# Modulation rows 2 to 8 summed along the row on VectorE, in a hybrid encoder layer on one core

## The chip, the cores and the metric

The kernel runs on one core of a Trainium2 chip. The metric is the device time of one execution in microseconds; the median of several executions is compared.

## The reference

One layer of an encoder is computed for two request groups that share all weights: 1024 prompt rows and 32 sample rows, 1056 in all, of 1024 features each. Everything is fp32.

```python
mod = (silu(c) @ w_ada + b_ada).reshape(B, 9, D_MODEL)[:, None]     # one c per group
modulate = lambda h, k: h * (1.0 + mod[:, :, 3*k + 1]) + mod[:, :, 3*k]
gate = lambda k: 1.0 + mod[:, :, 3*k + 2]
f = swiglu(modulate(x, 0), ffn1_w1, ffn1_w3, ffn1_w2)               # 1024 -> 2816 -> 1024
x = layer_norm(ALPHA * x + 0.5 * gate(0) * f, ln_g[0], ln_b[0])
proj = modulate(x, 1) @ w_in                                        # mixer: RG-LRU and spatial gating
...
x = layer_norm(ALPHA * x + gate(1) * m, ln_g[1], ln_b[1])
f = swiglu(modulate(x, 2), ffn2_w1, ffn2_w3, ffn2_w2)
x = layer_norm(ALPHA * x + 0.5 * gate(2) * f, ln_g[2], ln_b[2])
```

`mod` has nine sets of 1024 numbers for each group ("rows" 0 to 8). Rows 0 and 1 are needed before FFN 1, row 2 (a gate) when the first output of FFN 1 is added, rows 3 to 8 only later. `w_ada` has 1024 x 9216 numbers.

## The kernel before

Features lie on the 128 partitions (8 blocks of 128), the 1056 rows along the free axis in three chunks of 384, 384 and 288. To keep fp32 accuracy, each weight and each activation is split into a high and a low part (`split`, L208: ACT copies the high part, DVE or POOL subtracts it for the low part), and each product is made of three matmuls (high by high, high by low, low by high). `mm` (L151) issues every matmul and adds its modelled time to the kernel's own account `self.pe` (columns divided by 2.4 GHz). Only TensorE's order is the program's own; the other engines' orders are made by the scheduler, from the program order and what is ready.

FFN 1 has 22 tiles of 128 hidden features. For a plain tile `H` (L780) computes both input products over 8 feature blocks and 3 chunks, 144 matmuls in all, and `glu_end` the gated product g. For tiles 11 to 21 of FFN 1 and 3 to 21 of FFN 2, `H_fast` (L853) makes the two 384-chunks with seven block products instead of eight (Strassen's scheme); the third chunk is plain. It needs the combinations T1, T2, T3 and T4 of the activations. `combs` (L827) forms T1 and T3, in FFN 1 on POOL, in FFN 2 on DVE, and T2 on DVE; `comb_last` (L847) forms T4 on DVE. Each of them is four calls of `comb` (L815): three additions or subtractions, then a `split`. In `H_fast` T2 is used in the third product (S2), T1 in the fifth (S1), T3 in the sixth (S3), T4 in the seventh (A22). After the first product, ACT copies it out of PSUM (L875), because the fourth adds into the same bank; DVE's addition L868 must have read the S2 bank before S3 adds into it.

The tiles are taken in the blocks of `BLOCKS` (L47). After the tiles of a block, `F` (L1007) makes the output pass: for each of 8 feature blocks and 3 chunks one PSUM bank sums over the block's tiles (9 matmuls for each tile and feature block), and `add_gated` (L969) adds it, times the gate, to the residual on DVE: four instructions for each feature block, as the last chunk holds both groups. An output pass over n tiles has 72 n matmuls and 32 evictions. PSUM has eight banks, used in turn.

The hidden tiles g of a block stay in SBUF: tag "g" holds two, "tx" two (`tx` is also T1's and T3's place) and "t4" one.

Side work is written as generators that `go` (L155) puts in a list; after each group of matmuls `poll` (L161) continues those whose due time on `self.pe` is reached: a generator yields the time after which it wants to go on. `ada_rest` (L685) is the one for rows 2 to 8. It runs from the first matmul of tile 1. For each row it takes two halves of 512 output features. A half has four loads of 512 KB (`araw`, on the SP queue, in the same five slots as the weights), with an input feature to a partition. DVE multiplies each 512 columns by the partition's silu(c) and adds them up (L760, L762: 16 instructions for both groups). `sums` (L699) splits the sum, and TensorE adds up the 128 partitions with two matmuls a group (`psm`). `out` copies the two rows out of PSUM on ACT and writes them to DRAM, `back` reads them back turned, with a feature to a partition, and `use` adds the bias and makes the coefficients. The second step of one half is interleaved with the products of the next. `ffn` (L1025) makes sure that row 2 is done before the first output pass, and starts `combs` behind that pass in the program.

Of the kernel before, what the change touches and what calls it, by code (L numbers as in the profile page):

```python
# [12 lines left out]
F32 = mybir.dt.float32  # L13
F32R = mybir.dt.float32r
AF = mybir.ActivationFunctionType
ALU = mybir.AluOpType
# [30 lines left out]
BLOCKS = {1: [[0, 1, 2, 3, 4], [5, 6, 7], [8, 9, 10]] + [[b, b + 1] for b in range(11, 19, 2)] + [[19, 20, 21]],  # L47
# [76 lines left out]
class Core:  # L124
# [560 lines left out]
    def ada_rest(self):  # L685
# [4 lines left out]
        def raw(n):  # L690
            if n < 56 and n not in raws:
                r = self.wpool.tile([P, 2, 512], F32, tag="raw", name="araw", bufs=RAWS)
                nc.sync.dma_start(r, self.i["ada1"][n])
                raws[n] = r


        rows, pre = {}, None

        def sums(v, acc, ps):  # L699
            hl = [self.apool.tile([P, 512], F32R, tag="tot", name="acchl", bufs=self.ntot) for _ in range(2)]  # L700
            V.tensor_copy(hl[0], acc[:, v, :])
            V.tensor_tensor(hl[1], acc[:, v, :], hl[0].bitcast(F32), ALU.subtract)
            yield
            yield
            for q in range(2):
                self.mm(ps[0:2, :], self.one_r[:, v, :], hl[q], v + q == 0, v + q == 2)

        def out(m, h, ps):
            d = rows[m, h] = self.dram.tile([2, 512], F32, name=f"mrow{m}_{h}")
            row = self.apool.tile([P, 512], F32, tag="tot", name="row", bufs=self.ntot)[0:2, :]  # L710
            nc.scalar.activation(row, ps[0:2, :], AF.Copy)
            nc.scalar.dma_start(d, row)

        def back(m, h):
            with nc.allow_non_contiguous_dma(reason="a kilobyte of modulation, turned"):
                for v in range(2):
                    nc.sync.dma_start(self.mod[:, m, 4 * h:4 * h + 4, v],
                                        rows[m, h][v].rearrange("(f p) -> p f", p=P))

        def use(m, h):  # L720
            mod = self.mod[:, m, 4 * h:4 * h + 4, :]
            self.late = V.tensor_tensor(mod, mod, b_ada[:, m, 4 * h:4 * h + 4].unsqueeze(2).to_broadcast([P, 4, 2]), ALU.add)
            if h < 1:
                return
            self.mods.add(m)
            s = m // 3
            if m % 3 == 2:
                f = 0.5 if s != 1 else 1.0
                V.tensor_scalar(self.gt[:, s, :, :], self.mod[:, m, :, :], f, f, ALU.mult, ALU.add)
# [3 lines left out]

        def after(m, h, acc):

            ps = self.ps("psm")
            yield from sums(0, acc, ps)
            yield from sums(1, acc, ps)
            yield
            out(m, h, ps)  # L740
            yield
            back(m, h)
            yield
            use(m, h)

        raw(0)
        yield 1.0
        for i in range(14):
            m, h = 2 + i // 2, i % 2
            w = 2.3  # L750
            acc = self.gpool.tile([P, 2, 512], F32, tag="acc", name="acc", bufs=1)
            for q in range(4):
                n = i * 4 + q
                raw(n)
                r = raws.pop(n)
                for kk in range(2):
                    k = 2 * q + kk
                    for v in range(2):
                        if k == 0:
                            V.tensor_scalar(acc[:, v, :], r[:, kk, :], self.cs[:, k, v:v + 1], None, ALU.mult)  # L760
                        else:
                            V.scalar_tensor_tensor(acc[:, v, :], r[:, kk, :], self.cs[:, k, v:v + 1],  # L762
                                                   acc[:, v, :], ALU.mult, ALU.add)
                    yield w
                    if kk == 0:
                        raw(n + 1)
                    if pre:
                        next(pre, None)
            for _ in pre or ():
                yield w  # L770
            pre = after(m, h, acc)
            for _ in range(2):
                next(pre)
                yield w
            next(pre)
        for _ in pre:
            yield w
# [20 lines left out]
    def g_tag(self, nf, t):  # L798
        return "t4" if t == 2 or nf == 1 and t in (7, 10) else "tx" if t == LAST[2] or t in BLOCKS[nf][0][3:] else "g"
# [15 lines left out]
    def comb(self, dst, op, x, y, k, e):  # L815
# [5 lines left out]
        self.split(dst[0][:, k, :], dst[1][:, k, :], t, e)  # L821
# [5 lines left out]
    def combs(self, e):  # L827
# [5 lines left out]
        for k in range(4):  # L833
            self.comb(self.T1, ALU.subtract, B12, B11, k, e)
            yield 2.5 if e is V else 4.5
        self.T3 = self.tx_tile()
        for k in range(4):
            self.comb(self.T3, ALU.subtract, B22, B12, k, e)
            yield 2.5 if e is V else 4.5
# [693 lines left out]
INS = ["x", "vec", "wst", "ada0", "ada1", "lruw", "sgw", "sgb", "sglg", "sglb"]  # L1533
# [10 lines left out]
def layout(a):  # L1544
# [36 lines left out]
    for k in range(K):  # L1581
# [5 lines left out]
    ada1 = np.ascontiguousarray(  # L1587
        wa[:, 2 * D:].reshape(4, 2, P, 7, 2, 512).transpose(3, 4, 0, 2, 1, 5).reshape(56, P, 2, 512))
    lruw = np.zeros((4, P, 2, P), np.float32)
    for q, nm in enumerate(("lru_wa", "lru_wx")):  # L1590
# [6 lines left out]
        "vec": vec, "wst": wst, "ada0": ada0, "ada1": ada1, "lruw": lruw,  # L1597
# [26 lines left out]
```

## Time and profile before

| | us |
|---|---|
| median of 3 runs | 1922.78 |
| lowest and highest | 1922.46, 1927.21 |
| the profiled execution | 1925.68 |
| its span, from the first to the last instruction | 1924.0 |

The profile is one execution, recorded by the hardware. The engines are PE (TensorE matmuls), PEld (its weight loads, beside the matmuls), DVE (VectorE), ACT (ScalarE), POOL (GpSimd) and SP (the queue that issues most DMAs). A busy share is of the span. Matmuls overlap one another, so the duration of a single one is longer than the distance to the next; in a row that stands for several instructions the time runs from the first start to the last end. Square brackets at the end of a row give the idle time of the engine just before and who ended it. The chain is the work that ended last, followed back from the end.

### The profile page before, as it was taken

The numbers are of one execution on the slowest core, as the hardware profiler recorded it, in microseconds if no ns is written. First come the engines' busy times: TensorE is split into PE (matmuls) and PEld (weight loads), VectorE is DVE, ScalarE is ACT, GpSimd is POOL, SyncE is SP. The second block draws the span as 40 slices with busy tenths as digits, with TensorE's granted clock in tenths as the row PEclk, the third lists the DMA queues.
The fourth block names the chain that finished last, engine by engine and source line by source line (L and its number), as shares of the span: only waits on it lengthen the run. The fifth ranks groups of instructions, "written<-read, shape, count | busy, mean of one in ns | idle before, by whom it ended". The sixth has DMA issues, their size and how long they took to land.

```text
span 1924.0 us, 28361 instructions
## 1 busy us (share of the span) xinstructions
PE 1864.6 (97%) x11458; PEld 1818.6 (95%) x11458; DVE 1274.8 (66%) x2282; ACT 674.0 (35%) x1188; POOL 431.9 (22%) x340
## 2 busy tenths in 40 slices
PE   6999999998999999989999999999999999999996
PEld 3899999998999999989889999999999999999996
DVE  6867788779955554773776557865545554555477
ACT  5541122122232233345643517532332233223324
POOL 2201060003334234022000000042334233423410
PEclk9999999999999999989999999999999999999998
DMA  7333334332211111212011311111120112011102
GB/s 278 121 121 109 100 121 130 123 111 66 88 66 35 54 45 45 77 74 99 14 45 40 146 44 45 45 45 45 45 66 31 58 44 67 23 55 57 44 1 91
DMA packets 53996, 140.16 MB, mean 73 GB/s; under 512 B 19148, under 2 KB 21836, under 8 KB 53096
## 3 DMA queue, kind: packets, MB, share of 16 engines
q1 hardware_dynamic: 51888, 129.04, 20.1%
q10 hardware_dynamic: 1976, 9.30, 1.2%
q8 instruction: 90, 1.47, 0.3%
q14 instruction: 42, 0.34, 0.1%
HBM read 129.53 MB, written 8.79 MB: 72 GB/s over the span
## 4 chain that ended last, share of the span: by engine, by line
PE 85%; DVE 10%; ACT 2%; issue 1%; POOL 1%; DMA 0%; SPq 0%; POOLq 0%; DVEq 0%; ACTq 0%
PE ps L152 82%; DVE acc L762 1%; PE psl L152 1%; DVE xl L548 1%; DVE xa L975 1%; PE psa L152 1%; PE psz L152 1%; PE psm L152 1%; DVE wh L210 0%; PE psg L152 0%; ACT t L538 0%; DVE tot L981 0%; DVE s L819 0%; DVE xb L1100 0%; DVE xh L547 0%
## 5 line engine op out<-in xcount | busy, mean ns | idle before, releaser
L152 PE MATMUL ps<-xh,wh 128*128 128x384 f32 (+1 forms) x4080 | 971.9, 321 | 7.5 <-ACT s L875 5.7
L152 PEld LDWEIGHTS ps<-xh,wh 128*128 128x128 f32 x4080 | 711.8, 189 | 13.3 <-ACT s L875 6.3
L152 PE MATMUL ps<-xl,wh 128*128 128x384 f32 (+1 forms) x2040 | 653.4, 320 | 3.2 <-DVE xl L548 3.0
L209 ACT ACTIVATE wh<-raw 128x512 fp32r<-128x512 f32 x420 | 261.7, 628 | 588.0 <-PE ps L152 488.7
L152 PE MATMUL ps<-g,wh 128*128 128x384 f32 (+1 forms) x2664 | 440.2, 324 | 1.9 <-DVE g L210 1.7
L152 PEld LDWEIGHTS ps<-g,wh 128*128 128x128 f32 x2664 | 431.7, 188 | 5.5 <-DVE g L210 2.1
L152 PEld LDWEIGHTS ps<-xl,wh 128*128 128x128 f32 x2040 | 385.2, 189 | 7.3 <-DVE xl L548 5.3
L210 DVE TENSOR_TENSOR wh<-raw,wh 128x512 fp32r<-128x512 f32 x283 | 200.7, 716 | 266.7 <-ACT wh L209 264.5
L210 POOL TENSOR_TENSOR wh<-raw,wh 128x512 fp32r<-128x512 f32 x137 | 197.1, 1441 | 322.3 <-ACT wh L209 322.2
L975 DVE SCALAR_TENSOR_TENSOR xb<-ps,gt,xb 128x384 f32<-128x384 f32 (+1 forms) x352 | 151.9, 486 | 87.4 <-PE ps L152 73.3
L762 DVE SCALAR_TENSOR_TENSOR acc<-araw,cs,acc 128x512 f32<-128x512 f32 x196 | 148.3, 808 | 19.5 <-DMA araw<-ada 19.4
L239 POOL TENSOR_TENSOR raw<-raw 128x512 f32<-128x512 f32 x30 | 42.6, 1422 | 442.0 <-DVE wh L210 289.8
L975 DVE SCALAR_TENSOR_TENSOR xa<-ps,gt,xa 128x384 f32<-128x384 f32 (+2 forms) x256 | 109.8, 484 | 33.4 <-PE ps L152 33.3
L152 PE MATMUL ps<-tx,wh 128*128 128x384 f32 x720 | 130.2, 336 | 0.0
L152 PEld LDWEIGHTS ps<-tx,wh 128*128 128x128 f32 x720 | 124.3, 188 | 0.4
L209 ACT ACTIVATE g<-s 128x384 fp32r<-128x384 f32 (+1 forms) x120 | 58.4, 493 | 143.3 <-DVE s L674 143.3
L868 DVE TENSOR_TENSOR s<-s,ps 128x384 f32<-128x384 f32 x120 | 66.3, 552 | 42.7 <-PE ps L152 42.7
L210 DVE TENSOR_TENSOR g<-s,g 128x384 fp32r<-128x384 f32 (+1 forms) x120 | 81.9, 688 | 18.6 <-ACT g L209 17.3
L669 ACT ACTIVATE s<-ps 128x384 f32<-128x384 f32 (+1 forms) x102 | 46.0, 454 | 109.5 <-PE ps L152 109.2
L562 POOL TENSOR_TENSOR r<-r,half 128x3 f32<-128x3 f32 x8 | 7.4, 926 | 309.9 <-DVE r L561 309.9
L152 PE MATMUL ps<-T,wh 128*128 128x384 f32 x360 | 68.2, 337 | 0.0
L152 PEld LDWEIGHTS ps<-T,wh 128*128 128x128 f32 x360 | 63.6, 188 | 0.2
(235 smaller groups left out, 1699.6 us busy)
## 6 DMA issues: line engine op xcount, KB each, us to landing
raw<-wst SPq DMA_DIRECT2D x156, 512.0 KB, 3.9
araw<-ada SPq DMA_DIRECT2D x56, 512.0 KB, 3.3
wnat<-ada SPq DMA_DIRECT2D x8, 512.0 KB, 9.6
raw<-ada SPq DMA_DIRECT2D x8, 512.0 KB, 3.2
xt<-x SPq DMA_DIRECT2D x7, 512.0 KB
sp<-xa ACTq DMA_DIRECT2D x2, 1536.0 KB, 5.0
xb<-sp ACTq DMA_DIRECT2D x2, 1536.0 KB
y<-xb SPq DMA_DIRECT2D x4, 768.0 KB, 3.2
```

Of the source, the lines that this page charges most:

```text
L152: self.nc.tensor.matmul(out, a, b, start=start, stop=stop, skip_group_check=True)
L209: self.nc.scalar.activation(dst_h, src, AF.Copy)
L210: (e or self.nc.vector).tensor_tensor(dst_l, src, dst_h.bitcast(F32), ALU.subtract)
L239: G.tensor_tensor(a["A21"], a["A11"], a["A21"], ALU.subtract)
L548: V.tensor_tensor(xl, tmp, xh.bitcast(F32), ALU.subtract)
L562: self.nc.gpsimd.tensor_tensor(out, out, self.half[:n, :w], ALU.pow)
L669: self.nc.scalar.activation(s, x[:, :n], AF.Silu)
L762: V.scalar_tensor_tensor(acc[:, v, :], r[:, kk, :], self.cs[:, k, v:v + 1], acc[:, v, :], ALU.mult, ALU.add)
L868: V.tensor_tensor(out, x, ps[:, :n], ALU.add)
L975: V.scalar_tensor_tensor(X[:, m, a + o:a + o + w], ps[:, o:o + w], self.gt[:, s, m, v:v + 1], X[:, m, a + o:a + o + w], ALU.mult, ALU.add)
```

## The change

The output features of rows 2 to 8 now lie on the partitions. `ada1` is laid out as 56 tiles of 128 output features by 1024 inputs, the rows of the transposed matrix. Both vectors c are loaded once, as a new input `crow`, to all partitions, into the two "t4" tiles, and ACT applies Silu. Then each tile takes one DVE instruction a group: it multiplies the tile by c along the row and writes the sum of the row straight into `mod` (`accum_out`); the products themselves go to a scratch tile or over the loaded tile. The steps are due after 1.8 us for row 2 and 2.6 us for the others. The column sums, their splits, the rows in DRAM and their way back are gone.

With "t4" taken, g of more than three tiles at a time has no place: FFN 1's blocks of plain tiles become [0, 1, 2] and pairs, as FFN 2's are, and the third g of the first block lies in "tx" in FFN 1. In `comb` the high part is copied by the engine that formed the sum (POOL or DVE) instead of ACT, and the POOL steps of `combs` are due after 5.5 instead of 4.5 us.

```diff
-BLOCKS = {1: [[0, 1, 2, 3, 4], [5, 6, 7], [8, 9, 10]] + [[b, b + 1] for b in range(11, 19, 2)] + [[19, 20, 21]],
+BLOCKS = {1: [[0, 1, 2]] + [[b, b + 1] for b in range(3, 19, 2)] + [[19, 20, 21]],
           2: [[0, 1, 2]] + [[b, b + 1] for b in range(3, 19, 2)] + [[19, 20, 21]]}
...
-                r = self.wpool.tile([P, 2, 512], F32, tag="raw", name="araw", bufs=RAWS)
+                r = self.wpool.tile([P, 1024], F32, tag="raw", name="araw", bufs=RAWS)
                 nc.sync.dma_start(r, self.i["ada1"][n])
                 raws[n] = r
-        rows, pre = {}, None
-        def sums(v, acc, ps):
...
+        cb = []
+        for v in range(2):
+            t = self.apool.tile([P, 4, 384], F32, tag="t4", name="cb", bufs=2).rearrange("p a b -> p (a b)")[:, 0:D]
+            nc.sync.dma_start(t, self.i["crow"][v].partition_broadcast(P))
+            nc.scalar.activation(t, t, AF.Silu)
+            cb.append(t)
+        raw(0)
+        yield 1.0
+        for m in range(2, 9):
+            w = 1.8 if m == 2 else 2.6
+            for f in range(K):
+                n = (m - 2) * K + f
+                raw(n)
+                r = raws.pop(n)
                 for v in range(2):
+                    p = self.gpool.tile([P, D], F32, tag="acc", name="prod", bufs=1) if v == 0 else r
+                    V.scalar_tensor_tensor(p, r, 1.0, cb[v], ALU.mult, ALU.mult, accum_out=self.mod[:, m, f, v:v + 1])
+                    yield w
+                    raw(n + 1)
+            mod = self.mod[:, m, :, :]
+            self.late = V.tensor_tensor(mod, mod, b_ada[:, m, :].unsqueeze(2).to_broadcast([P, K, 2]), ALU.add)
             self.mods.add(m)
...
     def g_tag(self, nf, t):
-        return "t4" if t == 2 or nf == 1 and t in (7, 10) else "tx" if t == LAST[2] or t in BLOCKS[nf][0][3:] else "g"
+        return ("tx" if nf == 1 else "t4") if t == 2 else "tx" if t == LAST[2] else "g"
...
         e.tensor_tensor(t, t, u, ALU.add)
-        self.split(dst[0][:, k, :], dst[1][:, k, :], t, e)
+        e.tensor_copy(dst[0][:, k, :], t)
+        e.tensor_tensor(dst[1][:, k, :], t, dst[0][:, k, :].bitcast(F32), ALU.subtract)
...
             self.comb(self.T1, ALU.subtract, B12, B11, k, e)
-            yield 2.5 if e is V else 4.5
+            yield 2.5 if e is V else 5.5
...
-    ada1 = np.ascontiguousarray(
-        wa[:, 2 * D:].reshape(4, 2, P, 7, 2, 512).transpose(3, 4, 0, 2, 1, 5).reshape(56, P, 2, 512))
+    ada1 = np.ascontiguousarray(wa[:, 2 * D:].T).reshape(56, P, D)
```

## Rows read from the trace of the kernel before

**Rows 1.** The page, part 1: busy time, share of the span, instructions.
```profile
PE 1864.6 (97%) x11458; PEld 1818.6 (95%) x11458; DVE 1274.8 (66%) x2282; ACT 674.0 (35%) x1188; POOL 431.9 (22%) x340
```
**Rows 2.** Busy time by stretch: PE, PEld, DVE, ACT, POOL; granted clock, DMA share, GB/s.
```profile
84.50:421.00 336.50, 336.04 (x2065) 329.49 (x2065) 256.18 (x438) 83.90 (x164) 39.10 (x33) 1.00 0.37 120
310.00:346.00 36.00, 36.00 (x224) 35.42 (x224) 32.87 (x67) 4.39 (x9) 0.00 (x0) 1.00 0.34 112
421.00:457.20 36.20, 35.95 (x222) 35.07 (x221) 36.20 (x67) 6.78 (x13) 9.97 (x7) 1.00 0.20 61
457.20:517.16 59.96, 52.55 (x305) 49.63 (x304) 56.87 (x98) 20.14 (x39) 21.63 (x15) 0.94 0.32 105
517.20:582.00 64.80, 64.80 (x407) 64.80 (x408) 39.20 (x88) 19.34 (x36) 21.64 (x16) 1.00 0.15 50
...
1200.00:1248.00 48.00, 48.00 (x316) 48.00 (x315) 40.19 (x78) 27.74 (x59) 1.53 (x1) 1.00 0.14 45
```
**Rows 3.** Column sums: all, those after 457 (PE, PEld, ACT), and the chain.
```profile
L152 PE MATMUL psm<-acchl,one_r x56: 388/395/628, 116.4 to 505.2; 128*2 128x512 f32 x56
...
457.20:517.20 60.00, 3.08 (x8) 0.66 (x8) 1.16 (x2) 0.94 0.32 105
...
116.52 0.46 PE psm L152 x2
...
122.72 22.82 PE ps L152 x141
```
**Rows 4.** PE in order of time: start, duration, instructions, idle before and releaser.
```profile
457.21 0.33 PE L152 MATMUL ps<-xh,wh 128*128 128x384 f32 x1
...
469.52 0.63 PE L152 MATMUL ps<-xh,wh 128*128 128x384 f32 x1 [4.80 <-ACT s L875]
...
535.46 0.34 PE L152 MATMUL ps<-xh,wh 128*128 128x384 f32 x1
...
600.49 0.34 PE L152 MATMUL ps<-xh,wh 128*128 128x384 f32 x1
```
**Rows 5.** ACT in order of time, in the first fast tile.
```profile
465.70 0.52 ACT L209 ACTIVATE T<-s 128x384 fp32r<-128x384 f32 x1 [3.99 <-DVE s L820]
...
468.98 0.49 ACT L875 ACTIVATE s<-ps 128x384 f32<-128x384 f32 x1 [0.36 <-DVE T L210]
```
**Rows 6.** DVE forms: count, ns shortest/median/longest, first and last start.
```profile
L762 DVE SCALAR_TENSOR_TENSOR acc<-araw,cs,acc x196: 736/746/1779, 91.4 to 498.5; 128x512 f32<-128x512 f32 x196
L760 DVE TENSOR_SCALAR acc<-araw,cs x28: 477/485/1519, 89.7 to 478.9; 128x512 f32<-128x512 f32 x28
L701 DVE CAST acchl<-acc x28: 412/421/1241, 105.7 to 502.9; 128x512 fp32r<-128x512 f32 x28
L702 DVE TENSOR_TENSOR acchl<-acc,acchl x28: 678/693/1579, 106.2 to 503.8; 128x512 fp32r<-128x512 f32 x28
...
L1299 DVE SCALAR_TENSOR_TENSOR xc<-t,d x4: 1256/1261/1264, 935.2 to 1045.1; 128x1060 f32<-128x1060 f32 x4
...
L1308 DVE TENSOR_TENSOR_SCAN d<-t,p x4: 2274/2290/2291, 944.6 to 1055.1; 128x1024 f32<-128x1024 f32 x4
...
L1310 DVE COPY st<-d x4: 127/127/132, 947.0 to 1057.4; 128x1 f32<-128x1 f32 x4
```
**Rows 7.** DVE in order of time, beside POOL (240 to 255) and without it.
```profile
240.20 1.69 DVE L975 SCALAR_TENSOR_TENSOR xa<-ps,gt,xa 128x384 f32<-128x384 f32 x4
...
254.71 1.39 DVE L702 TENSOR_TENSOR acchl<-acc,acchl 128x512 fp32r<-128x512 f32 x1
...
327.10 1.69 DVE L975 SCALAR_TENSOR_TENSOR xa<-ps,gt,xa 128x384 f32<-128x384 f32 x4
```
**Rows 8.** POOL in order of time: the first combinations.
```profile
159.20 1.17 POOL L819 TENSOR_TENSOR s<-xh,xh 128x384 f32<-128x384 f32 x1 [74.64 <-DVE g L210]
...
240.79 2.00 POOL L210 TENSOR_TENSOR tx<-s,tx 128x384 fp32r<-128x384 f32 x2 [55.14 <-ACT tx L209]
```
**Rows 9.** SP queue: the first loads for rows 2 to 8.
```profile
85.14 8.36 SPq L693 DMA_DIRECT2D araw<-ada  x3
```

More of the change, by code (lines that the diff above doesn't have):

```diff
@@ L691, in raw @@
             if n < 56 and n not in raws:
-                r = self.wpool.tile([P, 2, 512], F32, tag="raw", name="araw", bufs=RAWS)
+                r = self.wpool.tile([P, 1024], F32, tag="raw", name="araw", bufs=RAWS)
                 nc.sync.dma_start(r, self.i["ada1"][n])
                 raws[n] = r
-        rows, pre = {}, None
-        def sums(v, acc, ps):
[L700 to L715, printed above, removed]
-                for v in range(2):
-                    nc.sync.dma_start(self.mod[:, m, 4 * h:4 * h + 4, v],
-                                        rows[m, h][v].rearrange("(f p) -> p f", p=P))
@@ L720, in use @@
[L720 to L724, printed above, removed]
+        cb = []
[4 more added lines that the diff above has]
+            cb.append(t)
@@ L728, in use @@
                 f = 0.5 if s != 1 else 1.0
-                V.tensor_scalar(self.gt[:, s, :, :], self.mod[:, m, :, :], f, f, ALU.mult, ALU.add)
+                V.tensor_scalar(self.gt[:, s, :, :], mod, f, f, ALU.mult, ALU.add)
             if m % 3 == 1:
@@ L732, in use @@
                 self.resid_coef(s, self.v("ln_g", (s - 1) * 8, s * 8), self.v("ln_b", (s - 1) * 8, s * 8))
[L734 to L777, printed above, removed]
     def H(self, nf, t):
@@ L838, in combs @@
             self.comb(self.T3, ALU.subtract, B22, B12, k, e)
-            yield 2.5 if e is V else 4.5
+            yield 2.5 if e is V else 5.5
         while not self.b12_free:
@@ L1530, in ffn_second @@
         self.H_chunks(2, [0, 1], ln2, 2)
-INS = ["x", "vec", "wst", "ada0", "ada1", "lruw", "sgw", "sgb", "sglg", "sglb"]
+INS = ["x", "vec", "crow", "wst", "ada0", "ada1", "lruw", "sgw", "sgb", "sglg", "sglb"]
 OUTS = {"y0": (P, K, CH[0][1]), "y1": (P, K, CH[1][1]), "y2": (P, K, CH[2][1]), "st": (P, 4, 8), "vn": (NS, 512)}
@@ L1596, in layout @@
         "x": np.concatenate([f("x_prompt")[0], f("x_sample")[0]], axis=0),
-        "vec": vec, "wst": wst, "ada0": ada0, "ada1": ada1, "lruw": lruw,
+        "vec": vec, "crow": np.concatenate([f("c_prompt"), f("c_sample")], axis=0), "wst": wst, "ada0": ada0, "ada1": ada1, "lruw": lruw,
         "sgw": f("sg_w")[0].transpose(2, 0, 1).reshape(P, 512),
```

## The prediction

> **What bounds the kernel now.** I read the engines' busy time first: TensorE (PE) is busy 97% of the span, VectorE (DVE) 66% [rows 1]. So time comes only from TensorE work that goes away or from stretches in which TensorE is held up. Then the busy time by stretch [rows 2]: from 84.5 to 421 us PE has no idle time worth a name (336.04 of 336.50), although DVE works 256 us of it; the reader is to see that a DVE at 76%, even at 91% within one output pass (310 to 346), does not hold PE up. From 421 to 517 it is the other way round: DVE is busy 36.20 of 36.20 and 56.87 of 59.96, PE falls to 52.55 and its granted clock to 0.94, a mean of its two levels (2.4 and 1.2 GHz). After that PE is full again with DVE at 60%. So there are two places where this change can act: the column-sum matmuls inside a full PE, and the DVE-bound change from plain to fast tiles around 457 to 517.
>
> The span is 1924.0 us, the profiled run 1925.7, the median of the timed runs 1922.8. I sum on the profiled run and carry the difference over to the median, since the parts touched do not differ between them.
>
> **What is removed.** *Column sums.* 56 matmuls of 512 columns, in 28 pairs; a pair takes 0.46 us of PE's chain [rows 3]. 28 x 0.465 = **13.0 us**, all in stretches where PE is the bound or waits for its own order.
>
> *The DVE-bound stretch.* From the start of the first fast tile (457.21) to the start of the tile two later (535.46) PE takes 78.25 us; the next such period, with the same matmuls, takes 600.49 - 535.46 = 65.03 [rows 4]. The excess is 13.2 us; four of the column-sum pairs lie in it (8 matmuls [rows 3]), 1.9 us, counted already. 11.3 us remain. The largest piece is a wait of 4.80 us before 469.52 for ScalarE (ACT) [rows 4], followed by matmuls at a lower clock. The ACT rows say why: the copy of the product out of PSUM (L875) stood in ACT's queue behind copies of T4 (L209), and these waited 3.99 us for DVE [rows 5]. Two edits meet it. The split in `comb` moves from ACT to the engine that forms the sum, so L875 has no T4 copy ahead of it. And the rows are done earlier. A step of 2.6 us on the kernel's own TensorE account is 18 matmuls (2.64); 141 matmuls take 22.82 us [rows 3], 0.162 each, so a step lasts 2.91 us. 96 of them last 280 us, and row set 2 (16 steps of 1.8, 12 to 13 matmuls, 2.05 us) 33: from 91 us, where the first product starts [rows 6], the work is over at about 405, not 510, and is gone before 457.
>
> **What is added or moved on DVE.** *The row products.* 112 instructions of 128x1024 that also write a sum; no row shows this form. Plain ones of the same kind take 0.746 us at 512 and 1.26 at 1060 elements [rows 6], so 1.23 at 1024; a one-column instruction takes 0.13. I take 1.36, as the operation and operands are the same. The lower bound is 1.23. The far bound is the scan, which also carries a value along a 1024-element row: 2.29 [rows 6]. 112 x 1.36 = 152 us replace 196 x 0.746 + 28 x 0.485 + 28 x 0.421 + 28 x 0.693 = 191: 39 us less. *Two more output passes.* FFN 1 goes from eight blocks to ten; each block evicts 8 times four pieces of 1.69 us [rows 7], so 27 us more. *T copies.* 8 in FFN 1 at about 0.42 us (the cast row [rows 6]), 3.4 us. DVE's total is nearly level; what changes is where it lies.
>
> *A pass of two tiles* is 144 matmuls, 23.3 us. In it: evictions 13.5, 8 products 10.9, 4 splits of 0.69 (as L702, the same shape [rows 6]) 2.8: 27.2 us, 3.9 more than PE takes. PSUM has 8 banks and a bank is 6 matmuls, 0.97 us, here; with 3 in work 5 can lag, 4.9 us. So three such passes should pass with at most 1 us each; I take 1 in all. Their cover is that DVE is used only to some 70% in the tiles between.
>
> *The first pass* is now of three tiles, from about 131 us (two tiles of 144 matmuls after 84.5, where tile 1 begins) to 166. DVE: 13.5 + 12 x 1.36 + 6 x 0.69 = 33.9 of 34.9 us, like the pass from 310 to 346 that cost nothing [rows 2]. New is GpSimd (POOL): its first combination started at 159 [rows 8], as soon as scratch tiles were free, then stuck until 240, when the first pass gave up its "tx" tiles. With tile 2 alone in "tx" a slot is free at once, and no ACT copy interrupts POOL. So 15 POOL instructions can fall into the first pass. The rows show what that does: with POOL at work a DVE subtraction takes 1.39 instead of 0.69 us, while four evictions from PSUM take 1.69 us in either case [rows 6, 7]. By the rows, 15 x 0.7 = 10.5 us more DVE, 9.5 late at the end against 4.9 of slack: 0 to 5 us, I take 3.
>
> *The start.* Two 512 KB loads of c and two Silu on ACT stand ahead of the first product. The SP queue issued three such loads within 8.4 us from 85.14 [rows 9]. What hides them: tile 1 needs none of it. The gate row needed by the first eviction (about 137) is ready at 91 + 33 = 125. Queued behind the Silu on ACT are weight copies; 0 to 3 us, I take 1. *The last plain pass*, [9, 10], from about 422: evictions 13.5, splits 2.8, T2 with four times four instructions of 384 elements (0.63, that is 0.746 less 128 x 0.94 ns) and a copy 11.8, then T4 11.8. DVE would be done 17 us after the pass; S3 and A22, which wait for it, come 13 and 15 us into the tile (by the share of their matmuls in a tile of (65.03 - 23.3) / 2 = 20.9 us, an estimate). But T2's sums can begin before the pass, since DVE has room after 405. 0 to 4 us, I take 1. *FFN 2*: 16 copies of 0.42 go from ACT to DVE, which has 8 us free of 48 at 1200 while PE is full [rows 2]: nothing; without that cover, up to 7. The removed trips through DRAM free SP and ACT slots on which nothing late hung: nothing.
>
> **Sum.** 13.0 + 11.3 - (1 + 3 + 1 + 1) = 18 to 19 us. 1925.7 becomes 1907, the median 1922.8 becomes **1904**.
>
> **Rivals.** *A, the passes become DVE-bound.* If the products cost 1.6 us or POOL keeps colliding, each pass of two lags 6 us or more instead of 3.9, and three or four passes stall for 2 to 4 us each, at a falling clock. Of the 24 us some 8 to 14 are given back: about 1914. For it: 27.2 of 23.3 is over the edge already. Against: the 310 to 346 pass. *B, slower: the sum does not run at one element a step.* At 2.29 + 0.13 = 2.42 a product, 271 us. The other DVE work from 84.5 to 421 is 256 less twelve fourteenths of 191, 92, plus 27: 390 us for a stretch of 326 (336 without eleven halves' column sums). 64 us of stalls less 24: about 1960. It begins to hurt at (326 - 119) / 112 = 1.85 us a product and loses from 2.06. Against it: plain products with two SBUF sources take 0.94 us for each 1000 elements more, half of what the scan takes [rows 6]. [...] *C, the stretch after 457 stays slow*, because T4 on DVE alone takes the place of the ACT wait: only the 13 us less 6 remain, or less: about 1917, near no change.
>
> **How the numbers follow.** Forecast 0.58 (1896 to 1910), A 0.19 (1910 to 1920), C 0.10 (1914 to 1922), B 0.13 (above 1930). A measurement of this kernel tells 0.3% (5.8 us) from no change. Faster takes the forecast, nearly all of A and half of C: 0.77; same 0.10; slower 0.13. The range runs from the two gains in full with nothing given back (1898), less 4 for the spread of the runs, to the end of A and most of C, 1921; outside lie B, whose bound is the scan row, and a few hundredths.
>
> **What would show it.** Right: no "psm" rows; products of about 1.3 us that end near 405; PE without idle time from 131 to 420; 65 to 67 us from the first fast tile to the tile two later, with no wait for L875. Wrong: products over 1.85 us; PE waiting for DVE evictions (L975) in the passes at 131, 212, 281 and 351; a wait for T4 in the first fast tile; or a late gate row at 137.

## The result and the profile after

The changed kernel took 1904.32 us (median of 6 runs, 1902.73 to 1908.87), beside 1922.67 for the kernel before on the same chip (6 runs, 1921.74 to 1927.21). The ratio is 0.9904, with a 95% interval of 0.9887 to 0.992: faster by 18.4 us. The forecast was 1904.0. The profiled run took 1902.73 us with a span of 1901.0, 22.95 us less than the profiled run of before.

The first line is the engines' busy time on the page [rows 1]; the three others are busy time by stretch, with the columns of [rows 2], here cut at the changed kernel's own first fast tile and at the tile two later.

```profile
PE 1847.3 (97%) x11402; PEld 1808.9 (95%) x11402; DVE 1257.2 (66%) x2307; ACT 654.5 (34%) x1144; POOL 443.7 (23%) x348
...
84.50:421.00 336.50, 333.94 (x2066) 332.37 (x2066) 277.51 (x532) 76.71 (x146) 56.21 (x43) 1.00 0.41 135
421.00:449.68 28.68, 26.85 (x164) 25.87 (x162) 28.54 (x58) 3.69 (x7) 7.16 (x6) 1.00 0.00 1
449.68:514.72 65.04, 65.04 (x410) 65.04 (x409) 39.26 (x74) 19.34 (x36) 21.97 (x17) 1.00 0.15 49
```

The shares on the page hardly moved. The place moved: VectorE (DVE) does 277.51 us up to 421, where it did 256.18, and 39.26 in the first two fast tiles, where it did 56.87 in less time. TensorE (PE) is now full in those tiles, at a granted clock of 1.00 where it had 0.94.

PE in order of time: every instruction from 84.5 to 515 us with idle time before it (in brackets, with what ended it), and the two starts that bound the fast stretch.

```profile
85.06 0.40 PE L152 MATMUL ps<-xh,wh 128*128 128x288 f32 x1 [0.55 <-ACT s L669]
...
141.65 8.60 PE L152 MATMUL ps<-g,wh 128*128 128x288 f32 x52 [0.96 <-DVE xa L924]
...
216.78 1.28 PE L152 MATMUL ps<-g,wh 128*128 128x384 f32 x6 [0.30 <-DVE g L210]
218.22 6.96 PE L152 MATMUL ps<-g,wh 128*128 128x288 f32 x42 [0.16 <-DVE g L210]
...
288.59 11.58 PE L152 MATMUL ps<-g,wh 128*128 128x288 f32 x70 [0.59 <-DVE g L210]
...
426.83 1.00 PE L152 MATMUL ps<-g,wh 128*128 128x288 f32 x4 [0.41 <-DVE s L674]
428.13 1.28 PE L152 MATMUL ps<-g,wh 128*128 128x384 f32 x6 [0.30 <-DVE g L210]
430.53 19.31 PE L152 MATMUL ps<-g,wh 128*128 128x288 f32 x119 [1.12 <-DVE g L210]
...
449.68 0.33 PE L152 MATMUL ps<-xh,wh 128*128 128x384 f32 x1
...
514.72 0.34 PE L152 MATMUL ps<-xh,wh 128*128 128x384 f32 x1
```

From these starts and [rows 4] the 22.95 us are placed. The first fast tile starts at 449.68 in place of 457.21: 7.53 us. From there to the tile two later it takes 65.04 us in place of 78.25: 13.21. That is 20.74 by 514.72; the other 2.2 lie later and are no more than the runs of one kernel differ by. These are the pieces of one pair of executions; between the medians there are 18.4 us, so the pieces add up to some 4 us more than the usual gain.

The row work on DVE. The first four lines give count, ns shortest, median and longest, first and last start, as in [rows 6]; the next two are the same products in the table of costly groups between 84 and 560 us (busy time and mean ns, then idle time ahead and what ended it); the last is the closing operation in order of time.

```profile
L713 DVE SCALAR_TENSOR_TENSOR prod<-araw,cb x56: 1210/1222/2028, 89.0 to 396.2; 128x1024 f32<-128x1024 f32 x56
L713 DVE DVE_READ_ACCUMULATOR prod<-araw,cb x56: 75/82/86, 90.1 to 397.4; 128x1 f32 x56
L713 DVE SCALAR_TENSOR_TENSOR araw<-araw,cb x56: 1211/1224/1917, 90.9 to 397.5; 128x1024 f32<-128x1024 f32 x56
L713 DVE DVE_READ_ACCUMULATOR araw<-araw,cb x56: 76/82/86, 92.1 to 398.7; 128x1 f32 x56
...
L713 DVE SCALAR_TENSOR_TENSOR araw<-araw,cb 128x1024 f32<-128x1024 f32 x56 | 74.2, 1325 | 1.2
L713 DVE SCALAR_TENSOR_TENSOR prod<-araw,cb 128x1024 f32<-128x1024 f32 x56 | 72.1, 1287 | 32.7 <-DMA araw<-ada 32.4
...
398.78 0.18 DVE L717 TENSOR_TENSOR mod<-mod,vec 128x16 f32<-128x16 f32 x1
```

A product is two instructions, 1.22 + 0.08 = 1.30 us by the medians and 1.39 by the means (20 of the 112 run beside GpSimd (POOL) and take up to 2.03; the other 92 take at most 1.23). The last row is done at 399; before, the last column sum started at 505 [rows 3].

### The profile page after: what moved, and what is told of

It reads as the page before. It is cut to its first block, busy times and chain, and to the rows that moved or that the text cites. A ratio compares the mean times of both kernels' runs of the same rounds, so it can differ in the third digit from the quotient of the medians.

```text
span 1901.0 us, 28144 instructions
## 1 busy us (share of the span) xinstructions
PE 1847.3 (97%) x11402; PEld 1808.9 (95%) x11402; DVE 1257.2 (66%) x2307; ACT 654.5 (34%) x1144; POOL 443.7 (23%) x348
## 4 chain that ended last, share of the span: by engine, by line
PE 81%; DVE 10%; DMA 2%; ACT 1%; issue 1%; POOL 0%; POOLq 0%; DVEq 0%; ACTq 0%
PE ps L152 79%; DMA araw<-ada 2%; DVE araw L713 1%; DVE prod L713 1%; PE psl L152 1%; DVE xa L924 1%; DVE wh L210 1%; PE psz L152 1%; PE psg L152 0%; DVE g L210 0%; DVE tot L930 0%; DVE xb L1049 0%; ACT t L538 0%; DVE s L674 0%; DVE t L1060 0%
## 5 line engine op out<-in xcount | busy, mean ns | idle before, releaser
L152 PE MATMUL ps<-g,wh 128*128 128x384 f32 (+1 forms) x2880 | 472.8, 324 | 4.3 <-DVE g L210 3.0
L152 PEld LDWEIGHTS ps<-g,wh 128*128 128x128 f32 x2880 | 464.0, 188 | 8.6 <-DVE g L210 4.5
L924 DVE SCALAR_TENSOR_TENSOR xa<-ps,gt,xa 128x384 f32<-128x384 f32 (+2 forms) x320 | 136.6, 484 | 24.7 <-PE ps L152 24.2
L209 ACT ACTIVATE g<-s 128x384 fp32r<-128x384 f32 x129 | 62.7, 493 | 170.2 <-DVE s L674 170.1
L210 DVE TENSOR_TENSOR g<-s,g 128x384 fp32r<-128x384 f32 x129 | 86.1, 674 | 20.8 <-ACT g L209 19.5
L713 DVE SCALAR_TENSOR_TENSOR prod<-araw,cb 128x1024 f32<-128x1024 f32 x56 | 72.1, 1287 | 32.7 <-DMA araw<-ada 32.4
L669 ACT ACTIVATE s<-ps 128x384 f32<-128x384 f32 (+1 forms) x102 | 46.2, 453 | 120.7 <-PE ps L152 120.2
L713 DVE SCALAR_TENSOR_TENSOR araw<-araw,cb 128x1024 f32<-128x1024 f32 x56 | 74.2, 1325 | 1.2
```

Of the source, the lines that this page charges most:

```text
L152: self.nc.tensor.matmul(out, a, b, start=start, stop=stop, skip_group_check=True)
L209: self.nc.scalar.activation(dst_h, src, AF.Copy)
L210: (e or self.nc.vector).tensor_tensor(dst_l, src, dst_h.bitcast(F32), ALU.subtract)
L669: self.nc.scalar.activation(s, x[:, :n], AF.Silu)
L713: V.scalar_tensor_tensor(p, r, 1.0, cb[v], ALU.mult, ALU.mult, accum_out=self.mod[:, m, f, v:v + 1])
L924: V.scalar_tensor_tensor(X[:, m, a + o:a + o + w], ps[:, o:o + w], self.gt[:, s, m, v:v + 1], X[:, m, a + o:a + o + w], ALU.mult, ALU.add)
```

## The experiments

So the time is as forecast, and it went from the two places that the prediction named. What its terms are worth one by one is another question, since each was argued from the full kernel alone. Four parts can be taken apart: the split inside `comb` ("comb"), the column sums, the passes, and the products. The table has all runs; the ratio is to the kernel before on the same chip, and differences below go by the ratios where nothing else is said. "No sums" leaves out the matmuls of the column sums and nothing else of the row work; rows 2 to 8 are then not the sums.

| run | what it holds | median us | ratio, 95% interval |
|---|---|---|---|
| e1 | before + comb | 1924.59 | 0.9997, 0.9985 to 1.001 |
| e9 | before + comb with less scratch | 1926.17 | 1.0009, 0.9998 to 1.002 |
| e2 | before, no column sums | 1920.55 | 0.9972, 0.996 to 0.9984 |
| e10 | before, no sums + comb | 1926.16 | 1.0008, 0.9997 to 1.0019 |
| e5 | before + passes | 1947.03 | 1.0127, 1.0112 to 1.0142 |
| e11 | before, no sums + passes | 1936.63 | 1.0054, 1.0035 to 1.0072 |
| e12 | before, no sums + passes + comb | 1933.81 | 1.0043, 1.0026 to 1.0059 |
| e3 | changed, without comb | 1915.52 | 0.9944, 0.9928 to 0.9961 |
| e8 | changed, once more | 1905.27 | 0.9914, 0.9899 to 0.9929 |
| e6 | changed, gated products first | 1911.72 | 0.9940, 0.9925 to 0.9955 |
| e7 | changed, GpSimd one block later | 1908.64 | 0.9925, 0.9909 to 0.9942 |
| e4 | changed, each product twice | 1975.65 | 1.0263, 1.0247 to 1.0278 |

### What held up the first fast tile: e1, e9

The prediction's reading was that ScalarE's (ACT's) copies of T4 held up L875, so that taking them off ACT frees it. In the expectation below this reading is the rival.

```diff
-        self.split(dst[0][:, k, :], dst[1][:, k, :], t, e)
+        e.tensor_copy(dst[0][:, k, :], t)
+        e.tensor_tensor(dst[1][:, k, :], t, dst[0][:, k, :].bitcast(F32), ALU.subtract)
...
```

> The kernel before with one edit alone: the high part in comb is copied by the engine that formed the sum, not by ACT (and POOL steps due after 5.5). Theory (the DVE-bound stretch comes mainly from the row work that lasts to 510; the ACT queue is only where it shows): the wait of 4.80 us for L875 goes, but DVE is as full as before and PE then waits for DVE's additions and for T4: 3 to 5 us of the 11.3 are gained, the two-tile period from the first fast tile falls from 78.3 to about 74, total about 1919. Rival (head-of-line blocking in ACT's queue is the cause): the period falls to 67 to 68, 9 to 11 us are gained, total about 1912.

Neither: no change. PE in the first fast tile of e1, in order of time, then the copy that it waits for, on ACT (L875 of before is L876 here):

```profile
467.06 0.69 PE L152 MATMUL ps<-xh,wh 128*128 128x384 f32 x1 [4.21 <-ACT s L876]
470.32 0.59 PE L152 MATMUL psm<-acchl,one_r 128*2 128x512 f32 x1 [1.93 <-DVE acchl L701]
471.30 0.58 PE L152 MATMUL psm<-acchl,one_r 128*2 128x512 f32 x1 [0.39 <-DVE acchl L702]
...
466.52 0.49 ACT L876 ACTIVATE s<-ps 128x384 f32<-128x384 f32 x1 [2.94 <-DVE T L822]
```

ACT is free of T4 and still idles 2.94 us until DVE's T4 work (L822) is done: the copy writes into one of five scratch tiles `s`, and those are in use by T4. e9 takes that cause away too, with one scratch tile less in each combination:

```diff
-        t, u = self.new_s(), self.new_s()
+        t, u = self.new_s(), dst[1][:, k, :]
...
-        e.tensor_tensor(t, t, u, ALU.add)
+        e.tensor_tensor(t, t, u.bitcast(F32), ALU.add)
...
```

> The kernel before with the combination's split on its own engine and one scratch tile less in each combination (its second difference is written where the low part will stand), so that y0's copy on ScalarE finds a scratch tile without waiting for T4's work on VectorE. Theory (with the copies off ScalarE, y0's copy still waited 4.2 us for TensorE's next step, by the scratch tile alone): the wait goes and 3 to 4 us are gained, 1919 to 1920. Rival (VectorE has T4's 22 instructions and the row work queued ahead of y1's addition, and PSUM fills instead): the wait moves to that addition or to the next column sums: 1922 to 1924.

No gain here either: the wait moved, as the rival had it. The same views of e9:

```profile
464.12 0.44 PE L152 MATMUL ps<-xh,wh 128*128 128x384 f32 x1 [1.16 <-ACT s L876]
470.43 0.59 PE L152 MATMUL psm<-acchl,one_r 128*2 128x512 f32 x1 [5.52 <-DVE acchl L701]
471.41 0.59 PE L152 MATMUL psm<-acchl,one_r 128*2 128x512 f32 x1 [0.39 <-DVE acchl L702]
...
463.59 0.47 ACT L876 ACTIVATE s<-ps 128x384 f32<-128x384 f32 x1
```

The copy now starts without any wait, and PE stands still until 470.43 all the same, for the next thing that DVE owes it: the split of a row's sum, queued behind T4. The three waits come to 6.53 us in e1 and 7.07 in e9. The wait for L875 was only the first place where a full DVE (56.87 of 59.96 us [rows 2]) showed.

### The column sums alone: e2, e10

```diff
-            for q in range(2):
-                self.mm(ps[0:2, :], self.one_r[:, v, :], hl[q], v + q == 0, v + q == 2)
+            ps[v] = hl
...
```

> The kernel before without the 56 column-sum matmuls; the rows are then copied from the split tile instead of PSUM, so rows 2 to 8 are not the sums (the output differs by that). All else stays: products, splits, DRAM trips, blocks. Theory: the matmuls cost their 0.465 us a pair on PE, 13.0 us in all, total about 1910; the excess of the two-tile period stays at 11 us or so. Rival (some of it is hidden, above all the four pairs in the DVE-bound stretch, and DVE's wait for psm tiles is another cost): under 10 us gained, or over 15.

5.4 us of the 13.0 (3 to 8 by the interval). The 13.0 us of matmuls are gone, but PE now meets DVE earlier. Two waits of e2, in order of time (L874 is L875 of before):

```profile
310.83 1.37 PE L152 MATMUL ps<-g,wh 128*128 128x288 f32 x7 [3.08 <-DVE s L674]
...
481.91 0.69 PE L152 MATMUL ps<-xh,wh 128*128 128x384 f32 x1 [5.46 <-ACT s L874]
```

The first did not exist before, and the second stood at 4.80 [rows 4]. From 84 to 600 us PE's idle time is 14.5 us, where it was 8.1. The first fast tile starts at 447.50, 9.7 us earlier than before, but from there to the tile two later it takes 81.59 us, where it was 78.25. Work taken off PE became time gained here only in part, less than half of it by the ratio.

e10 is e2 with the edit of e1.

> The kernel before without its 56 column-sum matmuls (rows 2 to 8 are then not the sums) and with the combination's split on its own engine. The first alone gave 5.4 us, the second alone none. Theory (the combination's edit earns nothing while the passes are of five and three tiles, since GpSimd then works late, 159 to 283, beside tiles whose evictions are far apart): as without the sums alone, 1917 to 1919. Rival (its worth of some 8 to 11 us in the changed kernel was hidden in the old one behind TensorE's column sums): 1906 to 1911.

Slower than both expectations: the gain of e2 is gone. The two largest sums of PE's waits in e10 from 84 to 600 us, by what it waited for (us in all, times, longest):

```profile
PE ps L152 <- DVE s L868: 6.5, 3, 2.9
PE ps L152 <- ACT s L669: 5.3, 1, 5.3
```

The edit puts eight more copies on DVE and eight on POOL in FFN 1, and sixteen on DVE in FFN 2; as in e1, ACT's relief earns nothing. Why it costs as much as 7 us here is not settled.

### The passes alone: e5, e11, e12

e5 takes the line of BLOCKS and `g_tag` over, nothing else (tile 2 in "t4").

```diff
-BLOCKS = {1: [[0, 1, 2, 3, 4], [5, 6, 7], [8, 9, 10]] + [[b, b + 1] for b in range(11, 19, 2)] + [[19, 20, 21]],
+BLOCKS = {1: [[0, 1, 2]] + [[b, b + 1] for b in range(3, 19, 2)] + [[19, 20, 21]],
...
```

> The kernel before with one edit of the change, the passes (three tiles, then eight passes of two, as the changed kernel has them, with tile 2's product in the T4 buffers), and its rows, column sums and combinations left as they are. Theory, by the sum of the prediction: the two passes more bring 27 us of VectorE work into stretches where its products, copies and evictions already fill most of the time, so the last row ends some 20 to 30 us later than before, deeper among the fast tiles: slower than before by 8 to 16 us, 1931 to 1940. Rival: VectorE's idle time among the plain tiles (some 80 us) swallows the passes, and only their order changes: within 2 us of before.

24 us slower, above the theory's 8 to 16. PE's waits for the column sums in e5 (84 to 600 us; columns as above), and its busy time by stretch around the fast tiles:

```profile
PE psm L152 <- DVE acchl L701: 7.3, 4, 3.8
PE psm L152 <- DVE acchl L702: 4.1, 5, 1.0
...
440.00:520.00 80.00, 71.24 (x407) 66.82 (x406) 79.21 (x135) 21.49 (x40) 23.80 (x16) 0.94 0.24 80
```

11.4 us are waits of the column sums for DVE's splits: PE's order is the program's own, and a sum that isn't ready holds up everything behind it, here for up to 3.8 us at a time. e11 takes these sums out.

> The kernel before without its 56 column-sum matmuls (rows 2 to 8 are then not the sums) and with the changed kernel's passes. The passes alone cost 24 us, the sums alone gave 5.4 back. Theory (the passes' price goes by TensorE's own waits in its queue for the split sums of VectorE, 11.4 us, and the low clock after them): without the sums most of it goes, 1921 to 1928. Rival (the price is VectorE's 27 us themselves, since the rows end later among the fast tiles): 1939 to 1944.

It lands between the two: 14 of the 24 us go with the sums (11 by the medians), where the same edit gave 5.4 with the old passes. That is about what the matmuls themselves take. The waits are not saved but come at other places: from 84 to 600 us PE's idle time is 26.3 us in e11 and 21.4 in e5. The longest wait of e11 is for a gated product that stands behind row work on DVE, and the stretch after it (by stretch, columns as above) ran at half the granted clock (0.50). The last two rows are DVE in order of time just before that product.

```profile
230.48 1.41 PE L152 MATMUL ps<-g,wh 128*128 128x288 f32 x4 [10.41 <-DVE s L674]
...
230.00:234.00 4.00, 3.03 (x9) 2.60 (x10) 3.97 (x9) 1.32 (x3) 0.00 (x0) 0.50 0.66 194
...
220.93 2.74 DVE L761 SCALAR_TENSOR_TENSOR acc<-araw,cs,acc 128x512 f32<-128x512 f32 x4 [3.52 <-DMA araw<-ada]
...
227.23 2.74 DVE L761 SCALAR_TENSOR_TENSOR acc<-araw,cs,acc 128x512 f32<-128x512 f32 x4 [2.96 <-DMA araw<-ada]
```

So DVE is not full at this border. It stands idle itself, 3.52 and 2.96 us, because the row products ahead of the gated product in its queue wait for their loads. Why these loads come late is not taken apart here.

e12 adds comb to e11. What is left to the changed kernel is the form of the row products, with all that hangs on it: the splits, the rows' way through DRAM, and the pace of the steps.

> The kernel before without its 56 column-sum matmuls (rows 2 to 8 are then not the sums), with the changed kernel's passes and the combination's split on its own engine: what is left to the changed kernel is the product of a whole row in place of accumulations of 746 ns and their splits. Theory (VectorE's sum: 191 us of row work in place of 152, so the last row ends some 60 us later, among the fast tiles): 1916 to 1924, 12 to 20 us behind the changed kernel. Rival (what counts is that TensorE no longer waits for row work, by whatever instruction): within 4 us of the changed kernel, 1904 to 1909.

It is slower still than the theory's range, 8 us behind the kernel before and 25 to 27 us behind the changed one (1.0043 against 0.9914 and 0.9904). Its row work in the table of costly groups on DVE, 84 to 560 us, and the first and last start of its products (columns as in [rows 6]):

```profile
L761 DVE SCALAR_TENSOR_TENSOR acc<-araw,cs,acc 128x512 f32<-128x512 f32 x196 | 153.3, 830 | 26.1 <-DMA araw<-ada 26.0
L702 DVE TENSOR_TENSOR acchl<-acc,acchl 128x512 fp32r<-128x512 f32 x28 | 21.3, 760 | 0.8
L759 DVE TENSOR_SCALAR acc<-araw,cs 128x512 f32<-128x512 f32 x28 | 15.3, 574 | 5.9 <-DMA araw<-ada 5.7
L701 DVE CAST acchl<-acc 128x512 fp32r<-128x512 f32 x28 | 12.8, 456 | 0.3
...
L761 DVE SCALAR_TENSOR_TENSOR acc<-araw,cs,acc x196: 735/745/1784, 92.9 to 510.5; 128x512 f32<-128x512 f32 x196
```

Together 202.7 us, where the products and their reads take 74.2 + 72.1 + 112 x 0.08 = 155, so 47 us more DVE work. But this is not the only difference. The old row work also ends later, and that goes by its pace: in the kernel before, the halves start at 90, 118, 147, 176, 205 and 235 us, some 29 us each, which is ten steps of 2.91 us. It has about 140 such steps where the changed kernel has 112 products, and e12 keeps them. Up to 421 us DVE is as busy in e12 (276.36 us) as in the changed kernel (277.51), and yet PE stands still for 10.4 us there, not 2.6. So with passes, sums and comb alike, the new row products make the difference between losing 8 us and gaining 17 to 18, by less work and by an earlier end. No run gave the old products a faster pace, so how much of it that alone would have brought is open.

### What comb is worth in the changed kernel: e3

The changed kernel with the three lines of comb as they were (the split back on ACT, and POOL's steps due after 4.5 us, which is not told apart from it).

> The changed kernel with comb's split put back on ACT (POOL steps due after 4.5 again). Theory (row work that ends at 400 is what frees the stretch): T4's copies find a DVE with room, L875 waits under 2 us, the two-tile period from the first fast tile is 65 to 68, total 1904 to 1907. Rival (the ACT queue is the cause): the wait of 4 to 5 us for L875 comes back with the lower clock behind it, period 72 or more, total 1911 to 1915.

By the ratios comb is worth 6 to 8 us here (0.9944 against 0.9914 and 0.9904), and not where the prediction put it. Rows of e3 in order of time: first PE at the two starts of the fast stretch, then what happens around 225, ACT and DVE ahead of PE.

```profile
462.13 0.34 PE L152 MATMUL ps<-xh,wh 128*128 128x384 f32 x1
...
527.15 0.34 PE L152 MATMUL ps<-xh,wh 128*128 128x384 f32 x1
...
193.14 0.53 ACT L209 ACTIVATE tx<-s 128x384 fp32r<-128x384 f32 x1 [4.57 <-POOL s L768]
193.57 0.61 ACT L209 ACTIVATE wh<-raw 128x512 fp32r<-128x512 f32 x1
...
194.22 1.51 DVE L210 TENSOR_TENSOR wh<-raw,wh 128x512 fp32r<-128x512 f32 x1 [5.12 <-ACT wh L209]
...
220.85 1.23 DVE L713 SCALAR_TENSOR_TENSOR prod<-araw,cb 128x1024 f32<-128x1024 f32 x1 [2.94 <-DMA araw<-ada]
...
224.46 1.38 DVE L674 TENSOR_TENSOR s<-s,ps 128x384 f32<-128x384 f32 x3
...
225.06 3.26 PE L152 MATMUL ps<-g,wh 128*128 128x288 f32 x9 [5.27 <-DVE s L674]
```

The fast stretch takes 527.15 - 462.13 = 65.02 us, as short as with comb: the comb edit is not needed to free it. What comb saves lies earlier, where POOL forms T1 and T3. With the split on ACT, ACT's queue stops for POOL (4.57), a weight copy stands behind it, DVE's weight split waits 5.12 for that copy, and the row products behind it are late (one waits 2.94 for its load besides) at the next border, where the gated product (L674) stands behind them and PE waits 5.27. ACT waits 22.3 us in all for POOL in this way between 84 and 400; the changed kernel has no such wait. In the first pass, too, PE waits longer without comb: 3.26 us for an eviction at 144.15, where it is 0.96 with it. That the stop at 193 leads to the wait at 225 is read from the order of these rows, and no run isolates it. Such stops need not cost anything: the kernel before had 18.2 us of them, and e1, which takes them away, gained nothing.

### Is the little that was lost to be had back: e6, e7, e8

e6 raises the priority of the gated products, e7 starts POOL's combinations one block later, and e8 is the changed kernel as it is, for comparison.

```diff
 e6
-        for c in range(3):
-            self.glu_end(g, c, ss[c], ps[c][:, :CH[c][1]])
+        with self.tc.high_priority(offset=60):
+            for c in range(3):
+                self.glu_end(g, c, ss[c], ps[c][:, :CH[c][1]])
...
 e7
-            if nf == 1 and b == BLOCKS[nf][0]:
+            if nf == 1 and b == BLOCKS[nf][1]:
```

> The changed kernel with the gated products at the end of a tile given a higher priority than the row products queued on VectorE, so that a pass no longer waits for them behind a product that waits for its araw. Theory (order on VectorE at the border of tile and pass): the waits for g at 213, 284 and 424 us (0.46, 0.59 and 1.53 us) go, and the kernel is 1.5 to 3 us faster than the changed one, 1901 to 1903. Rival: the evictions behind them come later by as much and the waits turn up inside the passes: within 0.5 us of the changed one.

> The changed kernel with GpSimd's combinations T1 and T3 started one block later, so that none runs beside the first pass. Theory (the first pass's one wait, 0.96 us at 141.65, comes from products of 2.0 us beside GpSimd in place of 1.22): that wait goes and 1 us is gained, if the same products do not wait in the passes of two, where GpSimd then works: 1903 to 1904. Rival: the slow products move with GpSimd and cost the next passes as much or more: 1904 to 1908.

> The changed kernel once more, beside the three above on one chip, as their measure: 1904 us, a ratio of 0.990 to the kernel before; its waits for g at 213, 284 and 424 us and for an eviction at 141.65 as in its first profile.

e8 repeats the result and its waits. Neither of the others gains: e7 can't be told from e8 (0.9925 against 0.9914), and e6 is about 5 us slower (0.9940), which neither of its two expectations had. In e6 the waits of 0.46 and 0.59 us are gone, and there is one of 3.58, besides 0.85 and 0.92 in the first pass; the first row below is that one, the second the stretch after it. Ahead of it DVE, too, stands idle: a row product at 221.31, in front of the gated product, waits 3.01 us for its load. In e7 the first pass is free of waits (its stretch is the third row: PE 35.00 of 35.00), and POOL's work costs the next passes more: the last two rows are such a wait and the stretch after it.

```profile
223.06 2.30 PE L152 MATMUL ps<-g,wh 128*128 128x288 f32 x6 [3.58 <-DVE s L674]
...
223.00:226.00 3.00, 2.94 (x9) 2.63 (x10) 3.00 (x8) 1.32 (x3) 0.00 (x0) 0.50 0.00 0
...
131.00:166.00 35.00, 35.00 (x219) 35.00 (x218) 32.88 (x67) 4.30 (x8) 0.00 (x0) 1.00 0.43 145
...
230.28 6.56 PE L152 MATMUL ps<-g,wh 128*128 128x288 f32 x30 [1.91 <-DVE xa L924]
...
230.00:234.00 4.00, 3.72 (x14) 3.72 (x15) 4.00 (x9) 0.00 (x0) 3.94 (x4) 0.58 0.51 179
```

e6 changes more than the waits at the borders: its first pass has 0.85 and 0.92 us of waits where the changed kernel has one of 0.96. So it does not prove that the border can't be had cheaper, only that this edit moves the wait. No run here beat the changed kernel.

### The rival's price: e4

```diff
-                    V.scalar_tensor_tensor(p, r, 1.0, cb[v], ALU.mult, ALU.mult, accum_out=self.mod[:, m, f, v:v + 1])
+                    if v == 0:
+                        for _ in range(2):
+                            V.scalar_tensor_tensor(p, r, 1.0, cb[v], ALU.mult, ALU.mult, accum_out=self.mod[:, m, f, v:v + 1])
+                    else:
+                        q = self.gpool.tile([P, D], F32, tag="acc", name="prod", bufs=1)
+                        V.scalar_tensor_tensor(q, r, 1.0, cb[v], ALU.mult, ALU.mult, accum_out=self.mod[:, m, f, v:v + 1])
+                        V.scalar_tensor_tensor(p, r, 1.0, cb[v], ALU.mult, ALU.mult, accum_out=self.mod[:, m, f, v:v + 1])
```

> The changed kernel with each of the 112 row products issued twice (the second writes the same sum), so a row costs 2.6 us of DVE instead of 1.30: the price at which rival B was put, with nothing else changed. By the sum of the prediction DVE work up to the first fast tile is 119 + 112 x 2.6 = 410 us for 326, 84 us over, so the total should rise by some 60 to 85 us above 1904, to about 1975. If DVE has more room than the sum says, or the products are put off behind urgent work, it rises by under 30.

1975.65, as forecast. The products of e4 for the first group (count, ns shortest, median and longest, first and last start), and PE at its first fast tile:

```profile
L715 DVE SCALAR_TENSOR_TENSOR prod<-araw,cb x112: 1204/1218/2040, 88.5 to 477.9; 128x1024 f32<-128x1024 f32 x112
...
521.30 0.34 PE L152 MATMUL ps<-xh,wh 128*128 128x384 f32 x1
```

This bears out the price of rival B at one point, 2 x 1.30 = 2.60 us. The edges that the prediction set for it (pain from 1.85 us a product, loss from 2.06) were not measured. If each us over the edge costs one us, as the prediction has it, this run puts them at about 1.96 and 2.13 (an estimate: 71.3 and 53.0 us over the changed kernel and the one before, by 112 products).

e4 also settles when the fast stretch is slow: when the row work reaches into it, and not by how much row work there is. It has more row work on DVE than any other run, 224 x 1.30 = 291 us by the medians, but the work is done at 483, before the first fast tile, and from there to the tile two later e4 takes 65.03 us. The other runs agree. With the old row products (before, e1, e2, e5 and e9 to e12) this period takes 77.55 to 83.15 us and the last row work ends inside it, at 503 to 521, whatever is done to passes, sums and comb. With the new ones (the changed kernel, e3, e4 and e6 to e8) it takes 65.02 to 65.04 and the row work ends ahead of it.

## Why the prediction was right, and where its working was not

*Right, with the size.* The fast stretch: forecast excess 13.2 us, measured gain 13.21, with no wait for the copy of L875. Of the two edits named for it only one was needed, as shown below. Up to the first fast tile, 24 of the 28 pairs of column sums, 11.2 us, less 6 for losses were forecast, so 5.2; it was 7.53. The difference is in the losses: PE's idle time from 84.5 to 449.68 is 2.56 + 1.83 = 4.4 us, and 0.7 was there before. In the sum, 18 to 19 forecast, 20.74 found by 514.72 in the profiled runs, 18.4 between the medians. That it comes so close is in part luck: the 6 to 8 us that comb is worth in the first passes stand in no term of the sum. The product was taken at 1.36 and took 1.30 (mean 1.39), from 89 to 399 us where 91 to 405 was said. The gate row was ready before the first eviction, and no wait there is to be seen.

*Rival B's condition.* It was a product of 2.42 us. Measured are 1.222 us for 1024 elements with the sum, and 0.082 for its read, where the plain form took 1.261 for 1060 [rows 6]. L1247 of the changed kernel, which has a single source, takes 0.706 us for 1060 elements. e4 shows that the price of rival B was about right; only its condition was not met.

*Wrong: why the stretch was slow.* The step "the largest piece is a wait ... for ACT" read the releaser of one wait as its cause and gave the comb edit a share of it. e1 removed that cause and e9 the next one, and the time did not move; e3 has the old comb and the stretch is full. What the three show, and e4 with them, is that DVE was the bound between 421 and 517, by T4 and row work at once, and that only the second of the "two edits", the earlier end of the rows, met it. [Rows 2] had said so by itself, with DVE at 56.87 of 59.96. The comb edit earns its 6 to 8 us elsewhere, in the first passes. The rows point to the hand-over between ACT and POOL there, which the prediction mentioned only as "no ACT copy interrupts POOL" and priced at nothing.

*Wrong: that the terms can be had one by one.* The sum set 13.0 for the column sums and counted the products and the two passes as nearly level on DVE. Both fit the whole change. Alone, the sums give 5.4 (e2) and the passes cost 24 (e5). Together with comb they lose 8 (e12), and the products then bring 25 to 27. The products, with their earlier end, are thus the largest part, and the sum had them as a side of a balance: 39 us less DVE work against 27 more. They also saved more than 39: the old instructions were priced by their medians (191 us), while in the trace of before they are busy 199.7, since some run slower beside POOL (L762 up to 1.78 us, where it takes at most 0.75 without POOL), and 155 took their place.

*The small losses.* The first pass: 3 us taken for POOL beside the evictions, 0.96 measured; in e7 without POOL it is 0. PE does not wait in the passes of two for evictions, as rival A had it, but at their borders for the gated products of the last tile (g, L674), 0.30 + 0.16 at 217 and 218, 0.59 at 289 and 0.41 + 0.30 + 1.12 from 427 to 431. The place was not foreseen; the size, 2.9 us against 2 taken for these passes and the last plain one, was about right. The start was put at 1 us: PE waits 0.55 at 85.06 for a copy on ACT (L669), and in e8 not at all. FFN 2 costs nothing that can be seen.

## What to carry to other kernels

When one engine is full, removing the wait that the trace names may only show the next one, as in e1 and e9 (0.9997 and 1.0009 of the time before); look at the busy share of the stretch first, and ask which edit takes work out of that engine there, if only by having it done earlier. Price the parts of a change both alone and together before calling them terms of a sum: here parts that lose 8 us together become a gain of 17 to 18 with one more. And an instruction that PE must run in order, but whose input comes from a busy engine, is where the delay shows: with DVE late, in e5, the column sums held PE up for 11.4 us, beside the 13.0 us that their matmuls take. Taking the sums out gave back about the matmuls alone (e11), since the late engine then held PE up elsewhere. DVE's queue does the same: at the border of a pass in e11 urgent work stood behind row products that waited 3.52 and 2.96 us for their loads.

## What the runs showed of the hardware

A row product that also sums is two instructions, 1.22 us for 128x1024 and 0.08 to read the accumulator. Both sources are fp32 in SBUF, and that is 1.19 ns an element, as in the plain product (1.26 us for 1060 elements). Beside POOL the product takes up to 2.03 us.

The granted clock has two levels in the profiles of before and of the changed kernel, 1.00 and 0.50. In before it is 0.50 from 472 to 475 us, and the 384-column matmuls there start 0.32 us apart, 1.2 columns a ns; at 1.00, from 449.68 in the changed kernel, they start 0.17 to 0.18 apart. Twice 1.2, for a granted clock twice as high, gives the 2.4 GHz of the prediction (an estimate).

A wait of PE can cost more than its length, where the clock behind it is lower. After waits of 3.58 us (e6) and 10.41 (e11) the granted clock was 0.50 in the next 3 to 4 us; after 1.91 (e7) it was 0.58 over 4 us, a mixture of the two levels. The length alone does not decide it: in the 3 us after the wait of 3.08 us in e2, and after one of 2.58 us at 505.78 in e11, the granted clock was 1.00 (as the means of 1.00 from 300 to 360 us in e2 and from 440 to 520 in e11 show). After the 1.12 us at 430.53 in the changed kernel the 119 matmuls behind it took 19.31 us, 0.162 each, the rate of the 141 in the prediction, at a granted clock of 1.00. So the changed kernel's short waits cost what they last, and the wait of 3.58 us in e6 about 1.5 us more in the 3 us behind it alone (an estimate: 9 matmuls there, 1.46 us at 0.162 each).
